# Two-layer hybrid decoder on one core: pools split over the two ends of SBUF, a seventh weight buffer, 384-column blocks second, and the first block's loads and sums in another order

## The chip, the core and the metric

One core of a Trainium2 chip runs the whole program in one launch. The metric is device time in microseconds (us), from one launch to its end. Single times of this kernel lie within about 0.06% of each other.

## What is computed

Two layers; in each, with x of 512 positions by 1024 channels in float32:

```python
for l in range(2):
    x = x + 0.5 * swiglu(rmsnorm(x, ln_ffn1[l]), w_ffn1_gu[l], w_ffn1_down[l])   # 1024 -> 2 x 2816 -> 1024
    h = rmsnorm(x, ln_mix[l])
    u_pool, q, k, v, gate_logits = split(h @ w_in[l])
    a = pool_mixer(u_pool, pool_w[l], pool_scale[l]) @ w_pool_branch[l]
    q, k = partial_rope(rmsnorm(q)), partial_rope(rmsnorm(k))                     # 8 heads, 2 kv heads, 64 wide
    b = swa_sink_attention(q, k, v, sinks[l]) @ w_attn_branch[l]                  # window 128
    x = x + (sigmoid(g_pool) * a + sigmoid(g_attn) * b) @ w_out[l]
    x = x + 0.5 * swiglu(rmsnorm(x, ln_ffn2[l]), w_ffn2_gu[l], w_ffn2_down[l])
```

## The kernel before, in words

Every large product is done with operands split into a high and a low part (ScalarE, called ACT, casts the high part; VectorE, called DVE, subtracts to get the low part), and three matmuls per term: high by high, high by low, low by high. x is held transposed, as eight tiles of 128 channels by 512 positions. A matmul has a stationary operand (loaded by the weight load, `PEld` in the profile) and a moving operand that streams past it; the profile writes `out<-moving,stationary`.

**Feed-forward (`ffn`, four times).** The gate and up projection is done in six blocks of columns, in the order of `GROUPS`: two of 384, two of 512, two of 512. After each pair comes `down`: the pair's rows of the second projection, for all eight output tiles. All blocks but the first of the program run `block`: a Strassen-like scheme with seven products ("a11", "a12", "a22", "s1" to "s4"), each of two chunks of weights. Combinations of activations (T1 to T4) sit in `xgh`/`xgl`, are stationary, and the weights `wh`/`wl` move. The order of products is `ORDER`, or `FIRST` for the first such block of a layer part, where "a11" is followed at once by "a12". After "a11", step `p1` copies the PSUM sums to `r`, because "a12" goes on adding into the same PSUM banks. `open_sums` lets DVE begin the weight sums for "s2". Results are turned by matmuls with the identity (`turned`: transposes into the PSUM banks `pt_tp` and `pt_pv`, then ACT writes `hh` and DVE `hl`); half of them are queued and turned in the next block by `turn`. In `down`, `wh`/`wl` are stationary and `hh`/`hl` move.

The very first block (`plain`) is an ordinary product of 384 columns in two halves j of four chunks. While x is still arriving, `split_plain` and the casts of the weight chunks alternate; `square` and `sums` make the norm; the combinations T1 to T4 (`first`, `others`) are made in the second half.

**Mixer (`mix`, twice).** 20 weight tiles for pool, keys and gates with `xgh`/`xgl` moving, then `br` (moving: `xgh`/`xgl`, where the pool result `ph`/`pl` lies in their spare columns, and the attention result `ah`/`al`) and `out` (moving: `yh`/`yl`). Attention and pooling run beside the gate tiles as generators; `HEADS`, `ATT` and `POOL` say at which half tile t each step of each generator is issued (odd t: after tile t//2 and its `prep`; even t: in the middle of a tile). `heads(b)` rotates q (DVE), transposes q and k into `pt_tp`/`pt_pv` (TensorE, PE), and copies them out to `kT` and `qT` (ACT). `attend` transposes its scores into `pt_tp` at its fourth step, half tile 4 + 3n + 5 for pair n.

**Queues and buffers.** Each engine works strictly in program order. Weights come through `Weights`: `load` issues a chunk's DMA on SyncE (SP) when the buffer six loads back (`RAW`) is free; "s1" and "s3" get a second, adding DMA from GpSimd (POOL). `prep`, after each chunk, makes high parts four chunks ahead and low parts three ahead.

**Addresses.** Pools are stacked upward from byte 8,320 of each partition, in the order they are opened. So, by their sizes, `wh` starts at 38,560, `wl` at 54,944, `xgh` at 83,616, `xgl` at 112,288 (to 140,960), the temporaries (`dh`, `dl` among them) at 145,088, `hh` at 164,672, `hl` at 181,056, `ah` at 179,008, `al` at 187,200, the ring of `yh`/`yl` at 195,648, and the `sums` buffers at 217,920 and 222,016. `pl` for k = 2 and 3 starts at 132,768 and 134,816. `wh`, `wl`, `xgh`, `xgl` start 32 bytes past a multiple of 64, the others named start on a multiple of 64.

Of the kernel before, what the change touches and what calls it, by code (L numbers as in the profile page):

```python
# [24 lines left out]
HT = S // 2  # L25
GROUPS = ((384, 384), (512, 512), (512, 512))
ORDER = ("a11", "s2", "s1", "s3", "a12", "s4", "a22")
# [14 lines left out]
RING = 16  # L42
RAW = 6
HI, LO = 4, 3
WARM = 20
KEYS = (-3,)
NORMS = (-2, -1, 1)
HEADS = ((0, 2, 2), (0, 3, 3), (3, 5, 5), (4, 6, 6))
ATT = tuple(tuple(4 + 3 * n + d for d in (0, 1, 2, 5, 6, 9, 10)) for n in range(8))
# [30 lines left out]


class InOrder:

# [18 lines left out]
def trunk(ctx, tc, xT, consts, vecs, rows, w_g4, w_g3, w_d8, w_d6, w_qkv, w_u, w_pool, w_gate, w_br, w_out, out):  # L102
    nc = Engines(tc)
    pool = lambda name, bufs, **kw: ctx.enter_context(tc.tile_pool(name=name, bufs=bufs, **kw))
    cp, rw, wh_, wl_, xp = pool("cp", 1), pool("rw", RAW), pool("wh", HI), pool("wl", LO), pool("xp", 1)
    tp, sp = pool("tp", TB), pool("sp", 2)
    pa = pool("pa", 1, space=PSUM)
# [43 lines left out]
    class Weights:  # L151
# [3 lines left out]
        def __init__(self):  # L155
            self.plan, self.loads, self.hi, self.lo = [], [], [], []
            self.at = self.loaded = self.summed = 0
            self.sums = None
            for l in range(L):
                for f in range(2):  # L160
                    if f == 1:
                        for kind, src, n in (("u", w_u[l], 2), ("qkv", w_qkv[l], 6), ("u", w_u[l, 2:], 2),
                                             ("gate", w_gate[l], 2 * KT), ("br", w_br[l], KT)):
                            for i in range(n):
                                self.add(kind, CH, src[i])
                        for m in HALVES:
                            self.add("out", CH, w_out[l, m])
                    b = 0
                    for gi, group in enumerate(GROUPS):
                        for i, n in enumerate(group):  # L170
                            w = w_g3[l, f, b] if n == 384 else w_g4[l, f, b - 2]
                            plain = l == f == 0
                            if plain and b == 0:
                                for j in range(2):
                                    for c in range(4):
                                        self.add("plain", 2 * n, w[j, c])
                            else:
                                self.block(w, 2 * n, FIRST if b == int(plain) else ORDER)
                            b += 1
                        last = gi + 1 == len(GROUPS)  # L180
                        for m in (HALVES if f == 1 and last else range(KT)):
                            w = w_d8[l, f, gi - 1, m] if gi else w_d6[l, f, m]
                            self.add("dn", 2 * sum(group) // 2, w)

# [7 lines left out]
        def block(self, w, n, order):  # L192
# [8 lines left out]
            for c in range(2):  # L201
                name["s2", c]["of"] = name["a11", c], name["s1", c]
                name["s4", c]["of"] = name["s2", c], name["a12", c]
                for k in ("a11", "s1", "a12"):
                    name[k, c]["uses"] += 1
            head = [name["s1", c] for c in range(2)]
            rest = [c for c in self.loads[first:] if c is not head[0] and c is not head[1]]
            self.loads[first:] = head + rest
# [45 lines left out]
        def low(self, upto):  # L254
            while len(self.lo) < min(upto, len(self.hi)):
                i = len(self.lo)
                c, n = self.plan[i], self.plan[i]["n"]
                self.lo.append(wl_.tile([P, CH], F32R, name="wl"))
                nc.vector.tensor_tensor(
                    out=self.lo[-1][:, :n], in0=c["raw"][:, :n], in1=self.hi[i].bitcast(F32)[:, :n], op=ALU.subtract  # L260
                )
                c["uses"] -= 1

        def prep(self):
# [55 lines left out]
    class Norm:  # L320
# [5 lines left out]
        def split(self, k, between=lambda: None):  # L326

            g = self.gain[:, k:k + 1]
            if self.h is None:
                self.h = xp.tile([P, 7 * 4 * HT], F32R, name="xgh")  # L330
                self.l = xp.tile([P, 7 * 4 * HT], F32R, name="xgl")
                self.spare = [t[:, KT * S:] for t in (self.h, self.l)]
# [45 lines left out]
        def split_plain(self, k, b12):  # L378
            g = self.gain[:, k:k + 1]
            if self.h is None:  # L380
                self.h, self.l = (
                    xp.tile([P, 7 * 4 * HT], F32R, name=n).rearrange("p (i k t) -> p i k t", i=7, k=4)
                    for n in ("xgh", "xgl")
                )
# [48 lines left out]
    def ffn(ctx, nm, nxt, last):  # L433
        hp = ctx.enter_context(tc.tile_pool(name="hp", bufs=1, reuse_waits="tile"))
        ep = ctx.enter_context(tc.tile_pool(name="ep", bufs=1, reuse_waits="tile"))
        er = ctx.enter_context(tc.tile_pool(name="er", bufs=2, reuse_waits="tile"))
        sums = ctx.enter_context(tc.tile_pool(name="sums", bufs=2, reuse_waits="tile"))
# [12 lines left out]
        def block(n, base, hid, order):  # L450
# [5 lines left out]
            def product(i, b, kind, go):  # L456
# [3 lines left out]
                for c in range(2):  # L460
# [9 lines left out]
                    if c == 0:  # L470
                        W.prep()
                after = go() if go else None
                W.prep()
# [5 lines left out]

            new = lambda name, pool=ep: [pool.tile([P, 512], F32, name=f"{name}{q}")[:, :n] for q in range(2)]  # L480
            r1, sa, u2, v = {}, {}, {}, {}
            rs = lambda b: nm.rstd[:, b:b + 1]

            def p1():
                r1.update(enumerate(new("r", er)))
                each(lambda q: nc.scalar.copy(out=r1[q], in_=pt[1][q]))

            def p2():
# [40 lines left out]
            for kind in order:  # L529
                i, b, go = steps[kind]  # L530
                product(i, b, kind, go)
                if kind in order[:2]:
                    turn()
            turns.extend((r1[q], q, base, n, hid, q) for q in range(2))
# [18 lines left out]
        def plain(n, base, hid):  # L553
# [4 lines left out]
            for k in range(KT):  # L558
                nm.split_plain(k, b12)
                if k % 2 == 0:  # L560
                    W.high(k // 2 + 1)
                    W.low(k // 2 + 1)
            for k in range(KT):
                nm.square(k)
            act = []
            for j in range(2):
                if j:
                    pts = pts[4:] + [pa.tile([P, S], F32, name=name)[:, :n] for name in ("pt_tp", "pt_pv")]
                for c in range(4):
                    wh, wl = (t[:, :2 * n].rearrange("p (k f) -> p k f", k=2) for t in W.take("plain"))  # L570
                    for k in range(2):
                        kt = 2 * c + k
                        for b in range(NB):
# [3 lines left out]
                            ah, al = (t[:, half if kt >= 4 else 0, cols] for t in a)  # L577
                            term(pts[b], kt, KT, ah, al, wh[:, k, :], wl[:, k, :])
                    if j == 0 and c == 3:
                        nm.sums()  # L580
                        for b in range(NB):
# [3 lines left out]
                            )  # L585
                    W.prep()
                    if j:
                        nm.first(c)
                        nm.others(c, nm.scaled(c + 4))
            for b in range(NB):  # L590
                u = (er if b < 2 else ep).tile([P, 512], F32, name=("r0", "r1", "v0", "v1")[b])[:, :n]
                nc.vector.scalar_tensor_tensor(
# [37 lines left out]

        for gi, group in enumerate(GROUPS):
            hid = [hp.tile([P, 8, S], F32R, name=n) for n in ("hh", "hl")]
            base = 0
            for i, n in enumerate(group):
                if nm is first and gi == i == 0:
                    plain(n, base, hid)
                else:
                    fresh = W.sums is None
                    if fresh:
                        open_sums()  # L640
                    block(n, base, hid, FIRST if fresh else ORDER)
                base += n // P
            final = gi + 1 == len(GROUPS)
            if final:
# [4 lines left out]
    @with_exitstack  # L649
    def mix(ctx, l, nm, nxt):  # L650
        mp = ctx.enter_context(tc.tile_pool(name="mp", bufs=1, reuse_waits="tile"))
        rp = ctx.enter_context(tc.tile_pool(name="rp", bufs=RING, reuse_waits="tile"))
        bank["mm"] = ctx.enter_context(tc.tile_pool(name="ps", bufs=4, space=PSUM, reuse_waits="tile"))
# [6 lines left out]
        us = [rp.tile([P, S], F32, name="u", tag="r") for _ in WIN]  # L660
        kv = mp.tile([P, NB, 4, HD], F32, name="kv")
        qT = mp.tile([P, G, S], F32, name="qT")
        kT = mp.tile([P, S], F32, name="kT")
        ph, pl = (t[:, :4 * S].rearrange("p (k t) -> p k t", k=4) for t in nm.spare)
        ah, al = (mp.tile([P, 4, S], F32R, name=n) for n in ("ah", "al"))
        nsink = sp.tile([P, HQ], F32, name="nsink")
# [30 lines left out]
        def rotate(z, n, cos, sin):  # L697
# [6 lines left out]
            nc.vector.tensor_tensor(out=z[..., 0:ROT], in0=ra, in1=rb, op=ALU.add)  # L704

        rs = mp.tile([P, NB, HQ], F32, name="hrs")

        ssq = mp.tile([P, NB, HQ], F32, name="hss")

# [38 lines left out]
        def heads(b):  # L748
# [13 lines left out]
            nc.scalar.copy(out=kT[:, sl], in_=pk[:, :P])  # L762
            nc.scalar.copy(out=qT[:, :, sl], in_=pt.rearrange("p (j t) -> p j t", j=G))
            yield

        def attend(b, jp):
# [8 lines left out]
            for j in range(2):  # L775
                for h, pr in enumerate(group):
                    nc.tensor.matmul(
                        sc[:, 2 * h + j, (0 if b else P):], qT[pr, 2 * jp + j, sl], kT[pr, lo:(b + 1) * P],
                        start=True, stop=True,
# [243 lines left out]
```

## Time and profile before

| | |
|---|---|
| median of 3 runs | 1951.1 us (1950.25 to 1951.4) |
| profiled execution | 1951.35 us, its span 1949.6 us |
| PE busy | 1921.7 us of the span |
| DVE, ACT, POOL busy | 1297.0, 844.3, 82.5 us |
| granted PE clock, mean | 0.995 |

The profile is one execution. Matmuls overlap in it: a matmul's listed duration is longer than the step from its start to the next one's start, so rates are read from starts. Busy time of an engine is the time in which any of its instructions runs. A wait is put down to the engine whose event came last.

### The profile page before, as it was taken

To read this page: it belongs to the slowest core of one execution; us is meant where nothing else is said; L and a number is where in the kernel's file an instruction comes from. 1 tells how busy PE (TensorE), PEld (TensorE's weight loads), DVE (VectorE), ACT (ScalarE), POOL (GpSimd) and SP (SyncE) were. 2 spreads that over 40 slices of the span, in tenths; PEclk is the share of its full clock that TensorE was granted. 3 is DMA by queue.
4 is the path that set the end of the run, shared out by engine and by line. 5 is a ranking of instruction groups with operands and counts; after the bars stand their busy time and mean duration, and the time that the engine had idled before them with its cause. 6 is when DMAs were issued, how large, how long until landed. Compare 5 with 4: busy or idle time off the path is not lost.

```text
span 1949.6 us, 24211 instructions
## 1 busy us (share of the span) xinstructions
PE 1921.7 (99%) x9264; PEld 1617.6 (83%) x9264; DVE 1297.0 (67%) x1896; ACT 844.3 (43%) x1282; POOL 82.5 (4%) x102
## 2 busy tenths in 40 slices
PE   8899999999999999999999999999999999999999
PEld 8788888897788988888889888888877879888887
DVE  5767476666657857648786684765765678575583
ACT  5435244445445534424454442443554455343351
POOL 0000000000000100000010000000000000000000
PEclk9999999999999999999999999999999999999999
DMA  5465563322223666456356655633212237664551
GB/s 184 125 176 168 137 176 120 106 93 77 76 86 77 164 162 182 130 148 176 108 128 164 177 159 121 187 116 100 87 65 86 87 75 185 163 184 141 151 162 44
DMA packets 76628, 256.13 MB, mean 131 GB/s; under 512 B 8640, under 2 KB 8896, under 8 KB 76512
## 3 DMA queue, kind: packets, MB, share of 16 engines
q1 hardware_dynamic: 62928, 209.48, 32.5%
q0 software_dynamic: 13296, 44.71, 13.7%
q8 instruction: 73, 1.20, 0.2%
q10 hardware_dynamic: 288, 0.39, 0.1%
q14 instruction: 43, 0.35, 0.1%
HBM read 252.45 MB, written 2.10 MB: 131 GB/s over the span
## 4 chain that ended last, share of the span: by engine, by line
PE 96%; DVE 2%; DMA 1%; ACT 1%; issue 0%; SPq 0%; ACTq 0%; DVEq 0%; POOLq 0%
PE mm L90 89%; PE sc L90 3%; PE pt_pv L90 2%; PE pt_tp L90 2%; DMA raw<-in_w_g 1%; DVE wl L90 0%; DVE t L90 0%; DVE xgl L90 0%; ACT wh L90 0%; ACT xgh L90 0%; DVE sums L90 0%; DVE r L90 0%; DVE x L90 0%; ACT xg L90 0%; DVE ssq L90 0%
## 5 line engine op out<-in xcount | busy, mean ns | idle before, releaser
L90 ACT CAST wh<-raw 128x1024 fp32r<-128x1024 f32 (+1 forms) x418 | 415.4, 994 | 529.1 <-PE mm L90 490.0
L90 DVE TENSOR_TENSOR wl<-raw,wh 128x1024 fp32r<-128x1024 f32 (+1 forms) x418 | 479.8, 1148 | 130.7 <-PE mm L90 87.6
L90 PE MATMUL mm<-wh,xgh 128*128 128x512 f32 (+2 forms) x1424 | 526.5, 370 | 16.1 <-ACT r L90 10.8
L90 PE MATMUL mm<-wl,xgh 128*128 128x512 f32 (+2 forms) x1424 | 523.7, 368 | 0.3 <-DVE wl L90 0.3
L90 PE MATMUL mm<-wh,xgl 128*128 128x512 f32 (+2 forms) x1424 | 523.6, 368 | 0.0
L90 PEld LDWEIGHTS mm<-wh,xgh 128*128 128x128 f32 x1424 | 270.4, 190 | 52.7 <-ACT r L90 12.2
L90 PEld LDWEIGHTS mm<-wl,xgh 128*128 128x128 f32 x1424 | 270.3, 190 | 35.8 <-DVE wl L90 0.7
L90 PEld LDWEIGHTS mm<-wh,xgl 128*128 128x128 f32 x1424 | 270.1, 190 | 35.0
L90 PE MATMUL mm<-hh,wh 128*128 128x512 f32 x704 | 281.1, 399 | 0.0
L90 PE MATMUL mm<-hl,wh 128*128 128x512 f32 x704 | 279.1, 396 | 0.0
L90 PE MATMUL mm<-hh,wl 128*128 128x512 f32 x704 | 279.0, 396 | 0.0
L90 DVE SCALAR_TENSOR_TENSOR x<-mm,x 128x512 f32<-128x512 f32 x96 | 66.3, 691 | 210.4 <-PE mm L90 210.3
L90 ACT CAST wh<-sums 128x1024 fp32r<-128x1024 f32 (+1 forms) x92 | 90.6, 985 | 173.8 <-PE mm L90 87.9
L90 PEld LDWEIGHTS mm<-hh,wl 128*128 128x128 f32 x704 | 132.6, 188 | 32.4
L90 PEld LDWEIGHTS mm<-hh,wh 128*128 128x128 f32 x704 | 132.6, 188 | 31.2
L90 PEld LDWEIGHTS mm<-hl,wh 128*128 128x128 f32 x704 | 132.6, 188 | 31.1
L90 PE MATMUL mm<-xgh,wh 128*128 128x512 f32 x384 | 154.7, 403 | 0.0
L90 POOL DMA_DIRECT2D raw<-in_w_g x92 | 79.4, 863 | 1773.5 <-DMA raw<-in_w_g 718.2
L90 PE MATMUL mm<-xgh,wl 128*128 128x512 f32 x384 | 150.1, 391 | 0.0
L90 PE MATMUL mm<-xgl,wh 128*128 128x512 f32 x384 | 149.9, 390 | 0.0
L90 DVE TENSOR_TENSOR wl<-sums,wh 128x1024 fp32r<-128x1024 f32 (+1 forms) x92 | 104.3, 1136 | 22.1 <-PE mm L90 22.1
L90 PEld LDWEIGHTS mm<-xgh,wh 128*128 128x128 f32 x384 | 72.1, 188 | 20.0 <-issue 5.6
(203 smaller groups left out, 1981.3 us busy)
## 6 DMA issues: line engine op xcount, KB each, us to landing
raw<-in_w_g SPq DMA_DIRECT2D x160, 512.0 KB, 3.6
raw<-in_w_g POOLq DMA_DIRECT2D x64, 512.0 KB, 6.6
raw<-in_w_d SPq DMA_DIRECT2D x64, 512.0 KB, 3.5
raw<-in_w_g SPq DMA_DIRECT2D x77, 384.0 KB, 3.7
raw<-in_w_gate SPq DMA_DIRECT2D x32, 512.0 KB, 3.5
raw<-in_w_d SPq DMA_DIRECT2D x32, 384.0 KB, 3.1
raw<-in_w_g POOLq DMA_DIRECT2D x28, 384.0 KB, 5.7
raw<-in_w_br SPq DMA_DIRECT2D x16, 512.0 KB, 3.4
```

What stands on the lines that cost most here:

```text
L90: return lambda *args, **kw: self.tc.keep_in_program_order(call(*args, **kw))
```

## The change

- The pools `wh`, `wl`, a new pool `xl` (with `xgh`, `xgl`) are stacked upward first ("left"), all others that live through the program downward from the upper end ("right"). `hp`, `ep`, `sums`, `ap`, `rp` and `mp` follow on the left. By the sizes, `wh` starts at 8,320, `wl` at 24,704, `xgh` at 36,992, `xgl` at 65,664, `hh` and `ah` at 94,336, `hl` at 110,720, `al` at 102,528, the `yh`/`yl` ring at 110,720 (its last six of 16 slots above 131,072). All of these start on a multiple of 64.
- `RAW` is 7. `er` goes: `r` has one buffer instead of two, and `turn` is called before `p1` instead of after it and its `prep`.
- `open_sums` is called at the end of `p1`, behind the copies to `r`, instead of before the block.
- In a `FIRST` block the loads of "a11" come first, then "s1"; before, "s1" came first.
- In all `ffn` but the first the two 384-column blocks come second.
- In `plain`, the first weight chunk is cast in two halves (`parts_of_first`), the norm's `sums` comes one chunk earlier, and the combinations are spread over both halves j (two `first` after each of chunks 0 and 1, then one `others` after each of the next four chunks).
- `qT` is one tile per block of 128 positions with two buffers, and `heads(2)` and `heads(3)` are issued later.

```diff
-RAW = 6
+RAW = 7
-HEADS = ((0, 2, 2), (0, 3, 3), (3, 5, 5), (4, 6, 6))
+HEADS = ((0, 2, 2), (0, 3, 3), (6, 9, 9), (12, 15, 15))
...
+def groups(start):
+    g = [(0, (384, 384)), (768, (512, 512)), (1792, (512, 512))]
+    return g if start else [g[1], g[0], g[2]]
...
-    cp, rw, wh_, wl_, xp = pool("cp", 1), pool("rw", RAW), pool("wh", HI), pool("wl", LO), pool("xp", 1)
-    tp, sp = pool("tp", TB), pool("sp", 2)
+    wh_, wl_, xl = pool("wh", HI, side="left"), pool("wl", LO, side="left"), pool("xl", 1, side="left")
+    cp, rw, xp = pool("cp", 1, side="right"), pool("rw", RAW, side="right"), pool("xp", 1, side="right")
+    tp, sp = pool("tp", TB, side="right"), pool("sp", 2, side="right")
...
-            head = [name["s1", c] for c in range(2)]
+            head = [name[k, c] for k in (("a11", "s1") if order is FIRST else ("s1",)) for c in range(2)]
...
+        def parts_of_first(self, k):
+            c = self.plan[0]
+            if k == 0:
+                self.hi.append(wh_.tile([P, CH], F32R, name="wh"))
+                self.lo.append(wl_.tile([P, CH], F32R, name="wl"))
+            cols = slice(k * c["n"] // 2, (k + 1) * c["n"] // 2)
+            split(self.hi[0][:, cols], self.lo[0][:, cols], c["raw"][:, cols])
+            c["uses"] -= k * 2
...
-        er = ctx.enter_context(tc.tile_pool(name="er", bufs=2, reuse_waits="tile"))
...
+                if kind in order[:2]:
+                    turn()
                 after = go() if go else None
                 W.prep()
...
             def p1():
-                r1.update(enumerate(new("r", er)))
+                r1.update(enumerate(new("r")))
                 each(lambda q: nc.scalar.copy(out=r1[q], in_=pt[1][q]))
+                if W.sums is None:
+                    open_sums()
...
                 product(i, b, kind, go)
-                if kind in order[:2]:
-                    turn()
...
                 nm.split_plain(k, b12)
-                if k % 2 == 0:
+                if k < 2:
+                    W.parts_of_first(k)
+                elif k % 2 == 0:
                     W.high(k // 2 + 1)
                     W.low(k // 2 + 1)
...
+            combos = [lambda j=j: nm.first(j) for j in range(4)]
+            combos += [lambda j=j: nm.others(j, nm.scaled(j + 4)) for j in range(4)]
...
+                    if j == 0 and c == 2:
+                        nm.sums()
+                    W.prep()
+                    for _ in range(2 if j == c // 2 == 0 else 1):
+                        if combos:
+                            combos.pop(0)()
                     if j == 0 and c == 3:
-                        nm.sums()
...
-                    W.prep()
-                    if j:
-                        nm.first(c)
-                        nm.others(c, nm.scaled(c + 4))
...
-                    fresh = W.sums is None
-                    if fresh:
-                        open_sums()
-                    block(n, base, hid, FIRST if fresh else ORDER)
+                    block(n, base, hid, FIRST if W.sums is None else ORDER)
...
-        qT = mp.tile([P, G, S], F32, name="qT")
+        qp = ctx.enter_context(tc.tile_pool(name="qp", bufs=2, reuse_waits="tile"))
+        qT = {}
...
+            qT[b] = qp.tile([P, G, P], F32, name="qT")
-            nc.scalar.copy(out=qT[:, :, sl], in_=pt.rearrange("p (j t) -> p j t", j=G))
+            nc.scalar.copy(out=qT[b], in_=pt.rearrange("p (j t) -> p j t", j=G))
```

More of the change, by code (lines that the diff above doesn't have):

```diff
@@ L25 @@
 HT = S // 2
-GROUPS = ((384, 384), (512, 512), (512, 512))
 ORDER = ("a11", "s2", "s1", "s3", "a12", "s4", "a22")
@@ L167, in __init__ @@
                             self.add("out", CH, w_out[l, m])
-                    b = 0
-                    for gi, group in enumerate(GROUPS):
+                    plain = l == f == 0
+                    for gi, (at, group) in enumerate(groups(plain)):
                         for i, n in enumerate(group):
-                            w = w_g3[l, f, b] if n == 384 else w_g4[l, f, b - 2]
-                            plain = l == f == 0
-                            if plain and b == 0:
+                            w = w_g4[l, f, (at - 768) // 512 + i] if at else w_g3[l, f, i]
+                            if plain and gi == i == 0:
                                 for j in range(2):
@@ L177, in __init__ @@
                             else:
[L178 to L183, printed above, removed]
+                                self.block(w, 2 * n, FIRST if 2 * gi + i == int(plain) else ORDER)
+                        for m in (HALVES if f == 1 and gi == 2 else range(KT)):
+                            w = w_d8[l, f, at // 1024, m] if at else w_d6[l, f, m]
+                            self.add("dn", sum(group), w)
         def add(self, kind, n, src=None, more=None, of=None):
@@ L205, in block @@
                     name[k, c]["uses"] += 1
-            head = [name["s1", c] for c in range(2)]
-            rest = [c for c in self.loads[first:] if c is not head[0] and c is not head[1]]
+            head = [name[k, c] for k in (("a11", "s1") if order is FIRST else ("s1",)) for c in range(2)]
+            rest = [c for c in self.loads[first:] if not any(c is h for h in head)]
             self.loads[first:] = head + rest
@@ L329, in split @@
             if self.h is None:
-                self.h = xp.tile([P, 7 * 4 * HT], F32R, name="xgh")
-                self.l = xp.tile([P, 7 * 4 * HT], F32R, name="xgl")
+                self.h = xl.tile([P, 7 * 4 * HT], F32R, name="xgh")
+                self.l = xl.tile([P, 7 * 4 * HT], F32R, name="xgl")
                 self.spare = [t[:, KT * S:] for t in (self.h, self.l)]
@@ L381, in split_plain @@
                 self.h, self.l = (
-                    xp.tile([P, 7 * 4 * HT], F32R, name=n).rearrange("p (i k t) -> p i k t", i=7, k=4)
+                    xl.tile([P, 7 * 4 * HT], F32R, name=n).rearrange("p (i k t) -> p i k t", i=7, k=4)
                     for n in ("xgh", "xgl")
@@ L478, in each @@
                 return [make(q) for q in range(2)]
-            new = lambda name, pool=ep: [pool.tile([P, 512], F32, name=f"{name}{q}")[:, :n] for q in range(2)]
+            new = lambda name: [ep.tile([P, 512], F32, name=f"{name}{q}")[:, :n] for q in range(2)]
             r1, sa, u2, v = {}, {}, {}, {}
@@ L585, in plain @@
                             )
-                    W.prep()
-                    if j:
-                        nm.first(c)
-                        nm.others(c, nm.scaled(c + 4))
             for b in range(NB):
-                u = (er if b < 2 else ep).tile([P, 512], F32, name=("r0", "r1", "v0", "v1")[b])[:, :n]
+                u = ep.tile([P, 512], F32, name=("r0", "r1", "v0", "v1")[b])[:, :n]
                 nc.vector.scalar_tensor_tensor(
@@ L629, in down @@
                 done(m, pd)
-        for gi, group in enumerate(GROUPS):
+        for gi, (_, group) in enumerate(groups(nm is first)):
             hid = [hp.tile([P, 8, S], F32R, name=n) for n in ("hh", "hl")]
@@ L637, in ffn @@
                 else:
-                    fresh = W.sums is None
-                    if fresh:
-                        open_sums()
-                    block(n, base, hid, FIRST if fresh else ORDER)
+                    block(n, base, hid, FIRST if W.sums is None else ORDER)
                 base += n // P
-            final = gi + 1 == len(GROUPS)
+            final = gi == 2
             if final:
@@ L650, in mix @@
     def mix(ctx, l, nm, nxt):
+        ap = ctx.enter_context(tc.tile_pool(name="ap", bufs=1, reuse_waits="tile"))
+        ah, al = (ap.tile([P, 4, S], F32R, name=n) for n in ("ah", "al"))
+        rp = ctx.enter_context(tc.tile_pool(name="rp", bufs=RING, reuse_waits="tile"))
         mp = ctx.enter_context(tc.tile_pool(name="mp", bufs=1, reuse_waits="tile"))
-        rp = ctx.enter_context(tc.tile_pool(name="rp", bufs=RING, reuse_waits="tile"))
         bank["mm"] = ctx.enter_context(tc.tile_pool(name="ps", bufs=4, space=PSUM, reuse_waits="tile"))
@@ L660, in mix @@
         us = [rp.tile([P, S], F32, name="u", tag="r") for _ in WIN]
-        kv = mp.tile([P, NB, 4, HD], F32, name="kv")
-        qT = mp.tile([P, G, S], F32, name="qT")
+        rs = mp.tile([P, NB, HQ], F32, name="hrs")
+        ssq = mp.tile([P, NB, HQ], F32, name="hss")
+        qp = ctx.enter_context(tc.tile_pool(name="qp", bufs=2, reuse_waits="tile"))
+        qT = {}
         kT = mp.tile([P, S], F32, name="kT")
         ph, pl = (t[:, :4 * S].rearrange("p (k t) -> p k t", k=4) for t in nm.spare)
-        ah, al = (mp.tile([P, 4, S], F32R, name=n) for n in ("ah", "al"))
+        kv = mp.tile([P, NB, 4, HD], F32, name="kv")
         nsink = sp.tile([P, HQ], F32, name="nsink")
@@ L704, in rotate @@
             nc.vector.tensor_tensor(out=z[..., 0:ROT], in0=ra, in1=rb, op=ALU.add)
-        rs = mp.tile([P, NB, HQ], F32, name="hrs")
-        ssq = mp.tile([P, NB, HQ], F32, name="hss")
         def sums(z, out):
@@ L777, in attend @@
                     nc.tensor.matmul(
-                        sc[:, 2 * h + j, (0 if b else P):], qT[pr, 2 * jp + j, sl], kT[pr, lo:(b + 1) * P],
+                        sc[:, 2 * h + j, (0 if b else P):], qT[b][pr, 2 * jp + j, :], kT[pr, lo:(b + 1) * P],
                         start=True, stop=True,
```

## The prediction

> **What bounds the kernel.** I read the page's busy times and chain first, then PE's list of waits, then the groups of matmuls by shape, then starts in the timeline.
>
> ```profile
> span 1949.6 us, 24211 instructions
> PE 96%; DVE 2%; DMA 1%; ACT 1%; issue 0%; SPq 0%; ACTq 0%; DVEq 0%; POOLq 0%
> ```
> ```profile
> PE mm L90 <- ACT r L90: 10.8, 4, 3.2
> PE pt_tp L90 <- DVE v L90: 6.4, 1, 6.4
> PE mm L90 <- ACT wh L90: 5.2, 1, 5.2
> ```
>
> PE is the chain: 96% of it. PE's waits come to about 24 us, nearly all in six places, and only the one at the very start has a transfer behind it. So two things can move the time: the step from one matmul to the next, and those six places.
>
> ```profile
> L90 PE MATMUL mm<-wh,xgh 128*128 128x512 f32 x896 | 350.0, 391 | 0.0
> ...
> L90 PE MATMUL mm<-hh,wh 128*128 128x512 f32 x704 | 281.1, 399 | 0.0
> ...
> L90 PE MATMUL mm<-xgh,wh 128*128 128x512 f32 x384 | 154.7, 403 | 0.0
> ...
> L90 PE MATMUL mm<-wh,xgh 128*128 128x384 f32 x432 | 149.3, 346 | 16.1 <-ACT r L90 10.8 <-ACT wh L90 5.2
> ...
> L90 PE MATMUL mm<-yh,wh 128*128 128x512 f32 x128 | 50.8, 397 | 0.0
> ...
> L90 PE MATMUL mm<-ah,wl 128*128 128x512 f32 x64 | 25.4, 398 | 0.0
> ```
>
> These give the counts (each stands three times: high by high, high by low, low by high). Listed durations overlap, so the step comes from starts. One tile of `br` holds the clean contrast:
>
> ```profile
> 544.76 0.39 PE L90 MATMUL mm<-xgh,wh 128*128 128x512 f32 x1
> ...
> 547.48 0.40 PE L90 MATMUL mm<-ah,wh 128*128 128x512 f32 x1
> ...
> 550.29 0.39 PE L90 MATMUL mm<-xgh,wh 128*128 128x512 f32 x1
> ```
>
> Twelve matmuls with `xgh`/`xgl` moving take 2.72 us, 226.7 ns a step; the next twelve, same shape, same weights, `ah`/`al` moving, take 2.81 us, 234.2 ns. All that differs is where the moving operand lies. Each step with `hh`, `hl`, `yh` or `yl` moving is like the second kind.
>
> **The change, part by part.**
>
> *1. Place of the operands.* 704 + 128 + 64 = 896 matmuls, times three = 2688 steps, at 7.5 ns (the difference above): 20.2 us, all on the path. But is it the place, and which property of it? The 128 KB line itself fits badly: `pl` for k = 2 and 3 starts at 132,768 and 134,816, above 131,072, and lies in the fast dozen. And a stationary operand costs too:
>
> ```profile
> 33.72 0.33 PE L90 MATMUL mm<-wh,xgh 128*128 128x384 f32 x1
> ...
> 34.76 0.34 PE L90 MATMUL pt_tp<-wh,sums 128*128 128x384 f32 x1
> ...
> 35.83 0.33 PE L90 MATMUL mm<-wh,xgh 128*128 128x384 f32 x1
> ```
>
> Six steps with `wh` moving and `xgh`/`xgl` stationary take 1.04 us (173.3 ns), six with the same `wh` moving and `sums` (at 217,920) stationary 1.07 us (178.3 ns). Three properties fit all these rows: a line near 140 KB for either operand; moving and stationary standing differently against multiples of 64 bytes (every slow pair has one on a multiple and one 32 bytes past it); or any operand on a multiple of 64. After the change all large operands lie under 143.5 KB and all on multiples of 64, so by the first two all pairs are fast, by the third all are slow. I take the gain; the third is a rival. A few steps are lost after each break by transposes, so I take 19.5 us. Bounds: nothing to 20.2, or a loss as below.
>
> [...]
>
> *2. Three later `ffn` starts.* One of three alike:
>
> ```profile
> 638.07 0.34 PE L90 MATMUL mm<-wh,xgl 128*128 128x384 f32 x1
> 641.62 0.69 PE L90 MATMUL mm<-wh,xgh 128*128 128x384 f32 x1 [3.22 <-ACT r L90]
> ...
> 644.96 0.34 PE L90 MATMUL mm<-wl,xgh 128*128 128x384 f32 x1
> ```
> ```profile
> 637.89 0.63 ACT L90 ACTIVATE sq<-x 128x512 f32<-128x512 f32 x1
> 640.36 0.83 ACT L90 CAST wh<-sums 128x768 fp32r<-128x768 f32 x1 [1.84 <-DVE sums L90]
> 641.10 0.85 ACT L90 COPY r<-mm 128x384 f32<-128x384 f32 x2
> ```
> ```profile
> L90 DVE TENSOR_TENSOR wl<-raw,wh 128x1024 fp32r<-128x1024 f32 (+1 forms) x418 | 479.8, 1148 | 130.7 <-PE mm L90 87.6
> ```
> ```profile
> 641.60:645.00 3.40, 3.38 (x11) 3.38 (x12) 1.28 (x2) 1.19 (x2) 0.86 (x1) 0.51 0.65 213
> ```
>
> "a12" waits for ACT's copies to `r`; ACT holds them behind `wh<-sums`, which waits for DVE's sum, and DVE is still at the norm. The gap costs 3.55 - 0.17 = 3.4 us. Then the granted clock is 0.51: ten matmuls in 3.34 us instead of 1.73, 1.6 more. With `open_sums` behind the copies, ACT can copy `r` as `sq` ends (638.5), and a 512-column "a11" ends 24 x (226.7 - 173.3) = 1.3 us later, at about 639.5: no gap. Late next are the sums of "s2" (DVE, about 1.15 us each, like a low part, and behind the norm): sum, cast, low part end about when "a12" does. I leave 0.2 us and take 3 x 4.8 = 14.4. Bounds: 0 to 15.
>
> [...]
>
> *3. The first 65 us.*
>
> ```profile
> 9.86 0.83 ACT L90 CAST wh<-raw 128x768 fp32r<-128x768 f32 x1 [5.18 <-DMA raw<-in_w_g]
> ```
> ```profile
> 19.80 5.46 DVE L90 TENSOR_TENSOR ssq<-ssq,sq 128x512 f32<-128x512 f32 x7
> ...
> 31.70 0.16 DVE L90 TENSOR_SCALAR rs_v<-pt_tp 128x4 f32<-128x4 f32 x1 [4.11 <-PE pt_tp L90]
> ...
> 33.88 0.16 DVE L90 SCALAR_TENSOR_TENSOR rstd<-rs_t,rstd 128x4 f32<-128x4 f32 x1
> ```
> ```profile
> 37.76 0.42 DVE L90 TENSOR_TENSOR d<-x 128x256 f32<-128x256 f32 x1
> ...
> 39.37 0.48 DVE L90 SCALAR_TENSOR_TENSOR t<-x,vec,xg 128x256 f32<-128x256 f32 x1
> ...
> 42.01 0.95 DVE L90 TENSOR_TENSOR wl<-raw,wh 128x768 fp32r<-128x768 f32 x1
> ```
> ```profile
> 57.37 1.14 DVE L90 SCALAR_TENSOR_TENSOR r<-mm,rstd,sa 128x384 f32<-128x384 f32 x2
> ```
> ```profile
> 52.35 0.34 PE L90 MATMUL mm<-wh,xgl 128*128 128x384 f32 x1
> 59.09 0.90 PE L90 MATMUL pt_tp<-cst,r 128*128 128x128 f32 x3 [6.40 <-DVE v L90]
> ```
>
> The halved first cast lets PE begin some 4 us sooner, but the norm's `sums` now stands a chunk earlier and PE must wait there for the squares (25.3), then at `pt_tp` until DVE reads the sums behind four `first`. So I expect "a11" to end near 52.3, as now. DVE is what counts: a `first` takes 1.6 us, an `others` 2.6, a low part 0.9, the norm's chain 2.4 with its start. From 25.3: four `first`, one low, the norm's chain, then four times low and `others`, two lows, and two results and a bit for `v` (1.7): 6.4 + 0.9 + 2.4 + 14.0 + 1.8 + 1.7 = 27.2, so 52.5 instead of 59.0. Then `turn` before the copies: transposes, two `hh` casts, the first copy of `r`, some 2 us, so "a12" at 54.4 instead of 61.8. With the slow-clock steps (1.4) gone and 0.4 for late sums: 7.4 + 1.4 - 0.4 = 8.4 us. Bounds: 3 to 10.
>
> *4. `heads(2)` and `heads(3)`.* At half tiles 9 and 15 they now meet the transposes of `attend` 0 and 2 in `pt_tp`:
>
> ```profile
> 432.44 0.60 PE L90 MATMUL pt_tp<-cst,q 128*128 128x128 f32 x4
> ...
> 432.91 0.47 PE L90 MATMUL mm<-xgh,wh 128*128 128x512 f32 x1
> ```
> ```profile
> 432.41 1.05 ACT L90 CAST wh<-raw 128x1024 fp32r<-128x1024 f32 x1 [1.78 <-PE mm L90]
> 433.37 0.26 ACT L90 COPY kT<-pt_pv 128x128 f32<-128x128 f32 x1
> 433.52 0.59 ACT L90 COPY qT<-pt_tp 128x512 f32<-128x512 f32 x1
> ```
>
> This is `heads(1)` now: PE goes on at 432.91, ACT has emptied `pt_tp` at 434.11, behind the weight cast. With `attend`'s transposes next in PE's queue, PE waits 1.2 us, and all gate tiles behind it. Four times: 5 us lost. Bounds: 0 to 7.
>
> *5. The rest.* The seventh buffer, the loads' order, 384 columns second, `turn` before `p1` in later blocks, one `r`: nothing. Their cover is that PE waits for no weights after the start; DVE is the engine that would show if it went: a low part late by its own length costs PE up to 1.15 us. Moves within DMA queues likewise: SP and POOL only issue loads.
>
> Sum, against this execution's 1951.35 us (span 1949.6, 0.25 above the median): 1951.35 - 19.5 - 14.4 - 8.4 + 5.0 = 1914.05. I say 1914.
>
> **The rivals.**
>
> *A: the place is not what costs*; the slow steps belong to the kind of stage. For: each slow kind has its own stage. Against: `br` alternates within one tile. 1914 + 19.5 = 1933.5. [...]
>
> *B, slower: multiples of 64 bytes are what costs.* Every slow row has such an operand and no fast one does; after the change all do. Then 896 + 384 matmuls with 512 columns, times three, at 7.5 ns (28.8) and 432 x 3 with 384 at 5.0 (6.5) slow down by 35.3 us, and the old slow ones stay: 1951.35 + 35.3 - 14.4 - 8.4 + 5.0 = 1968.9. It decides once these 5,136 steps lose more than 3.5 ns each (17.8 us over 5,136). Against: it makes the better aligned start the dearer one.
>
> *C: the waits are replaced.* ACT's copies of `r` now stand behind `turn` and late sums behind the copies; if half of parts 2 and 3 comes back: 1914 + 11.4 = 1925.4.
>
> **How the numbers follow.** My forecast 0.60 (own range 1904 to 1922: parts 3 and 4 at their bounds), C 0.13, A 0.17, B 0.10. Range 1902 to 1935: it takes in A and C and leaves B out. Faster by over 0.2% (about 4 us, the least this kernel's measurement tells from no change): the forecast, C and most of A, 0.87; same 0.03; slower 0.10.
>
> **What would show it.** Part 1: twelve steps of `ah` in 2.72 us, and the `hh` group's mean below 395 ns; if `xgh` steps go to 234, B. Part 2: no row "PE mm <- ACT r" over 1 us, and a clock of 1.00 at each `ffn` start. Part 3: first transposes of `r` near 52.5. Part 4: PE's waits list `pt_tp <- ACT qT`, four times, over 1 us each. What would make it wrong: B, or DVE falling behind in the 512-column blocks that now follow the norm.

## The result and the profile after

The changed kernel takes 1919.69 us, the median of four runs (1918.39 to 1920.03); the kernel before takes 1951.19 us beside it (1950.25 to 1951.4). The ratio is 0.9838, 95% interval 0.9821 to 0.9855: 31.5 us less. The profiled execution is the fastest of the four, 1918.39 us; the working below goes by it. The kernel before was also run seven times beside each batch of the experiments below: its medians there lie between 1949.87 and 1951.69 us, and the seven times of one batch up to 3.0 us apart, more than its first three. So a single time, or a comparison across batches, tells nothing below some 3 us.

The head of the page after, its busy times, and the line of the chain:

```profile
span 1916.6 us, 24198 instructions
...
PE 1897.8 (99%) x9264; PEld 1611.6 (84%) x9264; DVE 1296.1 (68%) x1897; ACT 843.2 (44%) x1283; POOL 82.5 (4%) x102
...
PE 95%; DVE 2%; ACT 1%; DMA 1%; issue 0%; SPq 0%; DVEq 0%
```

PE's list of waits after (sum, times, longest, in us):

```profile
PE pt_tp L95 <- ACT qT L95: 9.2, 4, 3.5
PE mm L95 <- ACT wh L95: 2.6, 1, 2.6
PE pt_pv L95 <- DVE warm_in L95: 1.1, 1, 1.1
PE pt_tp L95 <- DVE ssq L95: 1.0, 1, 1.0
PE mm L95 <- ACT r L95: 0.9, 1, 0.9
```

The two big rows of before (`r`, 10.8 us, and `v`, 6.4 us) are gone but for one copy of `r`. The longest wait is a new one, of `pt_tp` for `qT`. The groups of matmuls by shape:

```profile
L95 PE MATMUL mm<-wh,xgh 128*128 128x512 f32 x896 | 350.5, 391 | 0.0
...
L95 PE MATMUL mm<-hh,wh 128*128 128x512 f32 x704 | 276.3, 392 | 0.0
...
L95 PE MATMUL mm<-wh,xgh 128*128 128x384 f32 x432 | 146.5, 339 | 3.5 <-ACT wh L95 2.6 <-ACT r L95 0.9
...
L95 PE MATMUL mm<-yh,wh 128*128 128x512 f32 x128 | 49.8, 389 | 0.0
...
L95 PE MATMUL mm<-ah,wl 128*128 128x512 f32 x64 | 24.9, 389 | 0.0
```

`hh`, `yh` and `ah` as moving operands now cost what `wh` always did. In the timeline, of the tile of `br` that held the contrast (between the rows shown stand the other products of each dozen):

```profile
541.13 0.39 PE L95 MATMUL mm<-ah,wh 128*128 128x512 f32 x1
...
543.85 0.39 PE L95 MATMUL mm<-xgh,wh 128*128 128x512 f32 x1
...
546.57 0.39 PE L95 MATMUL mm<-ah,wh 128*128 128x512 f32 x1
```

Both dozens take 2.72 us, 226.7 ns a step.

Bookkeeping of the profiled execution, from starts. The steps with `hh`/`hl` moving sum to 496.43 us before and 481.32 after, `yh`/`yl` 89.97 and 87.04, `ah`/`al` 44.90 and 43.52: 19.4 us less. The first `down` starts 9.2 us sooner (the first start in the two rows below). Each of the three later `ffn` starts lost 3.4 us idle and some 1.6 in the slow clock before, and has no gap now: 14.9 less. The waits for `qT` cost 11 more. Together 32.5; the two executions differ by 33.0, so 0.5 us is left unassigned.

The `hh` group by tile, before and after (minimum, median and longest duration in ns, first and last start in us):

```profile
L90 PE MATMUL mm<-hh,wh x704: 392/397/482, 89.4 to 1945.0; 128*128 128x512 f32 x176
```
```profile
L95 PE MATMUL mm<-hh,wh x704: 388/389/477, 80.2 to 1912.0; 128*128 128x512 f32 x176
```

### The profile page after: what moved, and what is told of

It is laid out like the page before. It is cut to its first block, busy times and chain, and to the rows that moved or that the text cites. A ratio compares the mean times of both kernels' runs of the same rounds, so it can differ in the third digit from the quotient of the medians.

```text
span 1916.6 us, 24198 instructions
## 1 busy us (share of the span) xinstructions
PE 1897.8 (99%) x9264; PEld 1611.6 (84%) x9264; DVE 1296.1 (68%) x1897; ACT 843.2 (44%) x1283; POOL 82.5 (4%) x102
## 4 chain that ended last, share of the span: by engine, by line
PE 95%; DVE 2%; ACT 1%; DMA 1%; issue 0%; SPq 0%; DVEq 0%
PE mm L95 89%; PE sc L95 2%; PE pt_pv L95 2%; PE pt_tp L95 2%; ACT s L95 1%; DMA raw<-in_w_g 1%; DVE wl L95 0%; DVE m L95 0%; DVE s L95 0%; DVE ssq L95 0%; ACT wh L95 0%; DVE win L95 0%; DVE nm L95 0%; DVE z L95 0%; ACT qT L95 0%
## 5 line engine op out<-in xcount | busy, mean ns | idle before, releaser
L95 ACT CAST wh<-raw 128x1024 fp32r<-128x1024 f32 (+2 forms) x419 | 414.8, 990 | 491.2 <-PE mm L95 459.1
L95 DVE TENSOR_TENSOR wl<-raw,wh 128x1024 fp32r<-128x1024 f32 (+2 forms) x419 | 480.3, 1147 | 113.9 <-PE mm L95 73.7
L95 PE MATMUL mm<-hh,wh 128*128 128x512 f32 x704 | 276.3, 392 | 0.0
L95 PE MATMUL mm<-hh,wl 128*128 128x512 f32 x704 | 274.3, 390 | 0.0
L95 PE MATMUL mm<-hl,wh 128*128 128x512 f32 x704 | 274.0, 389 | 0.0
```

Source lines behind the costliest of these rows:

```text
L95: return lambda *args, **kw: self.tc.keep_in_program_order(call(*args, **kw))
```

## The experiments

### Which property of the place costs

Three pads shift `hh`, `ah`, the rings and `sums`, and leave `wh`, `wl`, `xgh`, `xgl` where the change put them. The floats per partition are 8, 16 and 32, which is 32, 64 and 128 bytes:

```diff
     wh_, wl_, xl = ...
     cp, rw, xp = ...
     tp, sp = ...
+    pad = pool("pad", 1, side="left").tile([P, 8], F32, name="pad")    # 16, 32
+    nc.gpsimd.memset(pad, 0.0)
```

The fourth kernel is the one before, with a pad that leaves everything high and only makes `hh`, `hl`, `ah`, `al` (and the `yh` ring, 256 bytes off by 512) stand like `wh`:

```diff
     tp, sp = pool("tp", TB), pool("sp", 2)
     pa = pool("pa", 1, space=PSUM)
+    pad = pool("pad", 1).tile([P, 216], F32, name="pad")
+    nc.gpsimd.memset(pad, 0.0)
```

32 bytes:

> The changed kernel with 32 unused bytes between xgl and the pools after it, so that hh, hl, ah, al, yh, yl lie 32 bytes higher, all still low, and 32 bytes past a multiple of 64 while wh, wl and xgh stay on one. If a line in the address decides (theory P), the steps with hh moving stay at 227 ns and the time at 1919 us. If the relative stand of moving and stationary operand decides (theory R), they go to 234 ns: 2688 x 7.5 ns = 20 us more, 1939 us.

64 bytes:

> The same with 64 unused bytes. Theory P: 1919 us. Theory R with a period of 64 bytes: 1919 us too, steps of 227 ns; theory R with a period of 128 bytes or more: 234 ns and 1939 us.

128 bytes:

> The changed kernel with 128 unused bytes in front of hh and the pools after it. 32 bytes made the hh steps 234 ns, 64 bytes some 230, and in the older layout 256 bytes (yh) left them at 227. If the period of the relative stand is 128 bytes: steps of 227 ns and 1919 us. If it is 256: slow steps again, 1927 us or more.

The kernel before, matched:

> The kernel before with 864 unused bytes behind its lasting pools: hh, hl, ah, al and the sums buffers stay high (165,536 and up) but now start 32 bytes past a multiple of 64 and at the same place in every 2 KB as wh, wl, xgh; yh and yl differ from wh by 256 bytes in every 512. Theory P: no change, 1951 us. Theory R: 2304 steps of hh, hl, ah, al go from 234 to 227 ns, 17 us less, 1934 us; the 384 steps of yh, yl go with them (2.9 us more) if the period is 256 bytes or a part of it.

| kernel | `hh` starts at | minus `wh`, modulo 256 | mean `hh`/`hl` step | us |
|---|---|---|---|---|
| before | 164,672 | 160 | 235.2 ns | 1951.19 |
| after | 94,336 | 0 | 228.0 | 1919.69 |
| pad of 32 | 94,368 | 32 | 234.3 | 1936.95 (one time) |
| pad of 64 | 94,400 | 64 | 229.9 | 1927.24 (one time) |
| pad of 128 | 94,464 | 128 | 234.0 | 1937.53 (one time) |
| before, matched | 165,536 | 0 | 227.9 | 1932.67 (1931.56 to 1932.71) |

(The mean of an undisturbed stretch is about 1 ns lower, since the `hh` steps contain the breaks.) The groups by tile, first of the kernel with the 32-byte pad, then of the matched one:

```profile
L95 PE MATMUL mm<-ah,wh x64: 394/396/400, 543.7 to 1541.2; 128*128 128x512 f32 x64
...
L95 PE MATMUL mm<-hh,wh x704: 393/396/485, 79.5 to 1930.6; 128*128 128x512 f32 x176
```
```profile
L90 PE MATMUL mm<-ah,wh x64: 389/389/390, 543.5 to 1536.7; 128*128 128x512 f32 x64
...
L90 PE MATMUL mm<-hh,wh x704: 388/389/477, 89.4 to 1926.4; 128*128 128x512 f32 x176
...
L90 PE MATMUL mm<-yh,wh x128: 388/389/390, 584.3 to 1580.2; 128*128 128x512 f32 x128
```

A shift of 32 bytes gives the loss back, far below 128 KB; the same operands at 165,536 and above are fast as soon as they stand like their partners. So it is not the height of the address, and not a line at 128 KB. (The trace after says the same by itself: the last six slots of the `yh` ring lie above 131,072, and no `yh` matmul in any slot is over 390 ns.) What counted in these six kernels is how the moving and the stationary operand stand to each other. The 128-byte pad is slow (234.0 ns), and the `yh` ring of the matched kernel, 256 bytes off, is fast (its matmuls last 389 ns in the median, against 397 before): this fits a period of 256 bytes. At 64 bytes neither of the two forecasts came (227 or 234 ns): the mean lies between, because two of every three steps take 229 to 232 ns (medians), while the third, with the low part `hl` or `yl` moving, stays at 226 (`yl` lasts 388 ns in the mean there, `yh` 394 and 392). The matched kernel against before: ratio 0.991 (0.9893 to 0.9926), 17.2 us below the kernel before beside it (1949.87), and 18.6 between the two profiled executions; by its steps 19.6, but its profile has more slow clock (0.992 in the mean, against 0.995). The pad of 32 adds 17.3 us to the changed kernel, and its steps with `hh`, `yh`, `ah` 13.3 + 2.6 + 1.3 = 17.2.

### The transposes of `heads(2)` and `heads(3)` in other banks

```diff
-            pt = pa.tile([P, S], F32, name="pt_tp")
+            pt = mm() if b > 1 else pa.tile([P, S], F32, name="pt_tp")
...
-            pk = pa.tile([P, S], F32, name="pt_pv")
+            pk = mm() if b > 1 else pa.tile([P, S], F32, name="pt_pv")
```

> The changed kernel with the transposes of heads(2) and heads(3) going to banks of the ring mm instead of pt_tp and pt_pv, so that the transposes of attend need not wait for ACT's copies. The four waits for ACT's copy to qT (9.2 us) should go, and the slow-clock stretch after one of them (about 1.7 us): 1909 us. If the wait turns up elsewhere (for mm, or for kT at the next product with v): 1914 us or more.

1906.57 us (1906.05 to 1907.29), ratio 0.9778 to the kernel before (0.9763 to 0.9792). The interval lies wholly below the change's own (0.9821 to 0.9855): of the kernels here this is the fastest, 13.1 us below the change in medians; as the kernel before was 1.3 us faster in this batch too, the 11.1 us between the two profiled executions is the better figure. Its waits list, from the top:

```profile
PE mm L95 <- ACT wh L95: 2.9, 1, 2.9
PE pt_pv L95 <- DVE warm_in L95: 1.1, 1, 1.1
```

The waits for `qT` are gone, and so is the stretch of slow clock behind the second of them. The windows view, the changed kernel's stretch behind that wait, and the same times here (busy time of PE, PEld, DVE, ACT, POOL, then granted clock, DMA share, GB/s):

```profile
465.40:469.00 3.60, 3.60 (x11) 3.02 (x12) 2.32 (x5) 1.28 (x4) 0.00 (x0) 0.53 0.41 135
```
```profile
465.40:469.00 3.60, 3.60 (x20) 2.70 (x17) 1.48 (x5) 2.09 (x6) 0.00 (x0) 1.00 0.45 146
```

### `open_sums` back ahead of the block

```diff
-                if W.sums is None:
-                    open_sums()
...
-                    block(n, base, hid, FIRST if W.sums is None else ORDER)
+                    fresh = W.sums is None
+                    if fresh:
+                        open_sums()
+                    block(n, base, hid, FIRST if fresh else ORDER)
```

> The changed kernel with open_sums back in front of the FIRST block, the rest as changed. If the order on ACT is what closed the gaps at the later ffn starts, they return: three waits of PE for ACT's r, each with a slow-clock stretch. With 512-column blocks a11 lasts 1.3 us longer than before, but the sums are longer too: 3 x 4 us, 1931 us. If the 512-column block alone had closed them: 1919 us.

1934.14 us (one time), 14.4 more than the change. The waits list and one of the places:

```profile
PE mm L95 <- ACT r L95: 10.6, 4, 2.8
```
```profile
635.90 0.50 PE L95 MATMUL mm<-wh,xgh 128*128 128x512 f32 x1 [2.75 <-ACT r L95]
```

The gaps are back, 3.13 us between starts at three `ffn` starts and 2.67 in the first. Of the 15.8 us between the two profiled executions, 11.9 come at the three later starts, 2.4 before the first `down` (82.57 instead of 80.20 us), and the rest, 1.5 us, in a slow-clock stretch of the second mixer (granted clock 0.995 in the mean, against 0.997 in the change). So it is the place of `open_sums` in ACT's queue that closes them.

### 384 columns first in every `ffn`

```diff
-    return g if start else [g[1], g[0], g[2]]
+    return g
```

> The changed kernel with the 384-column blocks first in every ffn, as before the change. My step 5 says nothing: 1919 us. The rival: with 384 columns a11 ends 1.3 us sooner, before ACT has copied r, and a wait of up to 1.3 us returns at each of three ffn starts: 1923 us.

1921.35 us (1919.93 to 1923.35), ratio 0.9844 (0.9827 to 0.986): not to be told from the change.

```profile
PE mm L95 <- ACT r L95: 2.5, 4, 0.9
```
```profile
631.10 0.44 PE L95 MATMUL mm<-wh,xgh 128*128 128x384 f32 x1 [0.53 <-ACT r L95]
```

The trace still shows what the order is for: half a microsecond at each of the three starts, which the longer "a11" of 512 columns covers. That is 1.6 us of the 14.9, under what the times can tell.

### The seventh buffer, and the order of the first loads

Six buffers with the changed order of loads, and six with the order of before:

```diff
-RAW = 7
+RAW = 6
```
```diff
-RAW = 7
+RAW = 6
...
-            head = [name[k, c] for k in (("a11", "s1") if order is FIRST else ("s1",)) for c in range(2)]
+            head = [name[k, c] for k in ("s1",) for c in range(2)]
```

Buffer alone:

> The changed kernel with six raw buffers, its new order of loads kept. With six buffers and the old order the time was 1925.9 us. If the missing buffer makes the late low parts at the ffn starts: some 1925 us again, the same six waits for DVE's low part. If the order of the loads made them: 1920 us.

Buffer and order:

> The changed kernel with six raw buffers and s1 ahead of a11 in the loads, both as before the change. My step 5 says nothing: 1919 to 1920 us. The rival: at the ffn starts the 512-column loads come late without them, and PE's waits list a cast or a low part waiting for a transfer, 1 us or more at each of three starts: 1923 us or more.

1924.68 us (1922.92 to 1925.78), ratio 0.9863 (0.9847 to 0.9879), and 1925.86 us (1925.47 to 1926.44), ratio 0.9872 (0.9855 to 0.9888). The runs of either lie above all of the change's (at most 1920.03), by 5.0 and 6.2 us in medians, though the intervals of the ratios overlap. With six buffers and the changed order, PE's waits and, in the timeline, ACT and PE at a start of `ffn`:

```profile
PE mm L95 <- DVE wl L95: 4.1, 7, 0.8
```
```profile
644.14 1.05 ACT L95 CAST wh<-raw 128x1024 fp32r<-128x1024 f32 x1 [7.22 <-DMA raw<-in_w_g]
...
653.77 0.50 PE L95 MATMUL mm<-wl,xgh 128*128 128x512 f32 x1 [0.42 <-DVE wl L95]
```

With six buffers a chunk's load arrives late, ACT casts it late (at 644.14, after 7.2 us of waiting for the transfer), DVE's low parts, which need these casts, and the sums between them then come one behind the other, and PE catches up with them in the later half of the first 512-column block (it runs from 624.75 to 664.4 us here). Six of the seven waits come in this block, at each of the three later `ffn` starts. Most of the loss comes with the buffer; the order of the loads (1.2 us between the two, in different batches) is not resolved.

### The first 65 us, part by part

The combinations back in the second half:

```diff
-                    for _ in range(2 if j == c // 2 == 0 else 1):
-                        if combos:
-                            combos.pop(0)()
+                    if j:
+                        combos[c]()
+                        combos[c + 4]()
```

> The changed kernel with the combinations back in the second half of the plain block, one first and one others after each of its chunks; the norm's sums stay a chunk earlier. If DVE's late work was the 6.4 us wait, PE waits for v again, 5 to 7 us, with a slow-clock stretch after it: 1926 us. If the earlier start of the kernel alone had closed it: 1919 us.

The norm's sums a chunk later, as before:

```diff
-                    if j == 0 and c == 2:
+                    if j == 0 and c == 3:
```

> The changed kernel with the norm's sums after chunk 3 again, the combinations spread as changed. The wait for the squares (1.0 us) goes, but the sums then stand behind one more others on DVE, and PE, which needs pt_tp in the second half, waits for them some 3 to 5 us: 1921 to 1924 us. The rival: the earlier place only costs, and without it the time falls to 1917 us.

The first chunk cast in one piece:

```diff
-                if k < 2:
-                    W.parts_of_first(k)
-                elif k % 2 == 0:
+                if k % 2 == 0:
```

> The changed kernel with the first weight chunk cast whole again. PE should then begin near 10.7 us instead of 5 us. My step 3 says that the earlier start is given back in the waits for the squares and for pt_tp, so the second block's a12 starts within 1.5 us of where it does now (53.8 us), 1920 us. The rival: the early start is kept, and without it everything is 4 us later: 1924 us.

One time each: 1928.75, 1925.33 and 1921.06 us. The line of PE's waits that tells each, in this order:

```profile
PE pt_tp L95 <- DVE v L95: 5.5, 1, 5.5
```
```profile
PE pt_tp L95 <- DVE rs_v L95: 5.3, 1, 5.3
```
```profile
PE mm L95 <- ACT wh L95: 5.5, 1, 5.5
```

And the slow clock that follows the first of them:

```profile
57.30:64.00 6.70, 5.41 (x18) 4.99 (x19) 5.49 (x8) 3.39 (x6) 0.00 (x0) 0.50 0.26 73
```

With the combinations in the second half, DVE is late with `v` as in the kernel before, and PE's clock is at half for two stretches: the first `down` starts at 88.28 us instead of 80.20, 8.1 us later. With the norm's sums a chunk later PE waits for DVE's `rs_v` earlier on, and the first `down` starts at 83.47, 3.3 us later; the rest of the 5.6 us above the median comes in slow-clock stretches of the two mixers (granted clock 0.995 in the mean, against 0.997), which this edit does not touch. With the first chunk cast whole PE's products start at 10.25 us; in the changed kernel they start at 5.13, and PE then waits 2.6 us behind 7.57. At the end one time shows no difference (1.4 us above the median), and "a12" starts at 54.1 instead of 53.84 us, the first `down` at 80.41 instead of 80.20: the early start is given back in waits.

## Why the prediction came out as it did

The forecast was 1914 us in 1902 to 1935, faster at 0.87; measured 1919.69. The mechanisms it named were those that act, and one term of the sum had the wrong size. The time lies inside the likeliest case's own range, 1904 to 1922, near its upper end. (That range's lower end does not follow from the bounds it names: parts 3 and 4 at their best give 1907.5.)

*Step 1, place of the operands: right.* 19.5 predicted, 19.4 measured. Of the three properties that it could not tell apart, the line near 140 KB falls (matched kernel), and so does "any operand on a multiple of 64", rival B: `wh` and `xgh` both stand on one now and the group stays at 391 ns. What is left is the second, the two operands standing differently, but it was drawn too narrowly: the pads of 64 and 128 bytes keep both on multiples of 64 and still cost, and 256 is the period that fits. Rival A (no place costs, 1933.5) falls too: the pad of 32 bytes alone takes 17.3 us.

*Step 2, the later `ffn` starts: right.* 14.4 predicted, 14.9 measured, and the kernel with `open_sums` put back loses 11.9 of it at these starts (one of its three gaps has no slow clock behind it, and "a11" is longer there). The 0.2 us that I left at each start did not come. The list shows one "PE mm <- ACT r" row, 0.9 us, under the 1 us named as the sign. Rival C fails here.

*Step 3, the first 65 us: right.* The path was foreseen: the early start is given back in waits, DVE decides. PE waited 2.6 us for the next cast behind 7.57 and 1.0 us for the squares behind 22.85; I had named the second, not the first, and the later wait that I had named as well, at `pt_tp` until DVE has read the sums, did not come. Two slow-clock stretches of 3.4 us, at 11.56 and 25.21 (granted clock 0.50 in both), I had not named either. They did not count: with 384 columns first in every `ffn` the profile has no slow stretch in the first 65 us, and there "a12" starts at 53.98. The return of PE:

```profile
51.82 0.55 PE L95 MATMUL pt_tp<-cst,r 128*128 128x128 f32 x3
...
53.84 0.45 PE L95 MATMUL mm<-wh,xgh 128*128 128x384 f32 x1 [0.95 <-ACT r L95]
```

Predicted 52.5 and 54.4. To the first `down` 9.2 us were won, predicted 8.4.

*Step 4, `heads(2)` and `heads(3)`: the term that was mis-sized.* Predicted 5.0 as four times 1.2 us; measured 9.2 us of waits, and 11 with the slow clock, above the bound of 7 that I gave it. The place, the engine and the four times are right. PE's timeline after, at half tile 15 of the first layer:

```profile
461.21 0.60 PE L95 MATMUL pt_tp<-cst,q 128*128 128x128 f32 x4
461.64 0.27 PE L95 MATMUL pt_pv<-cst,kv 128*128 128x128 f32 x1
...
465.40 1.03 PE L95 MATMUL pt_tp<-cst,s 128*128 128x128 f32 x4 [3.49 <-ACT qT L95]
```

And ACT in the same stretch:

```profile
461.14 0.49 ACT L95 ACTIVATE s<-s,nm,scale 128x128 f32<-128x128 f32 x1 [3.70 <-DVE nm L95]
...
463.16 0.60 ACT L95 CAST dh<-d 128x512 fp32r<-128x512 f32 x1
463.67 1.04 ACT L95 CAST wh<-raw 128x1024 fp32r<-128x1024 f32 x1
464.61 0.26 ACT L95 COPY kT<-pt_pv 128x128 f32<-128x128 f32 x1
464.77 0.58 ACT L95 COPY qT<-pt_tp 128x512 f32<-128x512 f32 x1
```

I took ACT's queue from `heads(1)`, where only a weight cast stands ahead of the copies; that holds at half tile 9 (1.1 us). At half tile 15 the queue still holds what was issued half a tile before: a step of attention, four exponentials that had waited for DVE's `nm` until 461.14, and a pooling cast `dh`. So it is 461.14 to 465.35 before `qT` is out, and two of the four waits are 3.5 us. I had read what these instructions cost, but not which generators issue just ahead of that place. In the first layer the granted clock was then 0.53 over 3.6 us, which I had priced for the `ffn` starts and not here. The kernel that moves these transposes to other banks wins 11.1 us by the profiles (13.1 in medians), where I had named 5.0.

*Step 5, "the rest nothing": half right.* 384 columns second and the loads' order are within what the times tell. The seventh buffer is not nothing: without it the change loses 5.0 us. I had named the cover (PE waits for no weights) and the engine that shows if it goes (DVE, a low part late by up to 1.15 us), but I priced the buffer against the kernel before, where 384-column blocks come first. In the order of the change the cover needs the buffer; which part of the new order makes it so is not shown, since six buffers were not run with the 384-column blocks first. In the sum the zero stood rightly, since buffer and order come together. `turn` ahead of `p1` and the single `r` were not run apart.

The errors against 1914.05 add up to 0.5 + 0.8 better and 0.1 + 6 worse, so 1918.9; the profiled execution took 1918.39.

## What to carry to other kernels

Where matmuls of one shape step at two rates in one trace, compare early on where the moving and the stationary operand start modulo 256 bytes, the period that fits here: a pad of a few bytes is a cheap edit, and it tells (32 bytes cost 17.3 us). A copy's price is what stands ahead of it in its engine's queue at that very place (PE waited 1.1 us for `qT` at half tile 9, 3.5 us at half tile 15), so list the instructions of every generator that issues there or just ahead, and do not take the price from a quieter place. A buffer priced at nothing against the order before can be what the new order rests on.

## What the runs showed of the hardware that I had not expected

- The step of a 512-column float32 matmul with a weight load of its own went, in the six kernels of the table, with where the moving operand stands relative to the stationary one: 226.7 ns where they differ by a multiple of 256 bytes and 234.2 at 160 bytes off (the `ah` dozens of after and before); with `hh`/`hl` moving, breaks included, 228.0 at 0, 234.3 at 32, 229.9 at 64, 234.0 at 128 and 235.2 at 160. Why is open: no run here looked at the weight load and the moving stream by themselves.
- In the profiles of before and after, the granted clock falls to 0.50 in stretches of 3.41 us, once of 6.83 (before, at 57.81 us); the last of either, 2.80 and 2.44 us, is cut short by the end. The length of a gap alone did not decide whether it cost a stretch: 3.76 us between starts in the first layer of the changed kernel was followed by half the clock, the same 3.76 us in the second layer was not (0.50 and 1.00 in the last row of each fence below); with `open_sums` ahead of the block the gap of 3.13 us at 977.1 us was followed by a slow stretch (steps of 0.43 us), the one at 632.8 was not (0.23). The stretches of one execution start whole multiples of 3.413 us apart (after: (465.53 - 11.56) / 133 = 3.413; before: (641.49 - 57.81) / 171 = 3.413 and (993.07 - 57.81) / 274 = 3.413), so their starts give a grid, and the two gaps of 3.76 us lie differently on it (windows view, columns as above):

```profile
462.12:465.53 3.41, 0.13 (x1) 0.13 (x2) 1.74 (x3) 3.23 (x10) 0.00 (x0) 1.00 0.00 0
465.53:468.94 3.41, 3.41 (x11) 2.83 (x12) 2.19 (x5) 1.28 (x4) 0.00 (x0) 0.50 0.42 136
```
```profile
1407.61:1411.02 3.41, 1.79 (x11) 1.31 (x9) 1.85 (x7) 2.39 (x10) 0.00 (x0) 1.00 0.27 109
1411.02:1414.44 3.42, 1.55 (x9) 1.37 (x10) 3.12 (x6) 2.17 (x6) 0.00 (x0) 1.00 0.00 0
1414.44:1417.85 3.41, 3.41 (x21) 2.09 (x19) 0.72 (x2) 0.93 (x4) 0.00 (x0) 1.00 0.47 154
```

  In the first layer PE is busy for 0.13 us of one cell of the grid, and half the clock follows; in the second layer the gap is shared by two cells, busy for 1.79 and 1.55 us, and the clock stays. In the profiles of before and after, between 60 and 1900 us, half the clock followed each of the four full-clock cells in which PE idled for 2.5 us or more (before 3.09, 2.66 and 2.50 us, in the cells from 638.08, 989.65 and 1600.64; after 3.28, in the cell from 462.12), and none in which it idled less (1.87 at most). So what goes with the clock here is how much of a gap falls in one cell, not its whole length. In the first 25 us after, a cell with 0.96 us of idle (from 21.80) was followed by half the clock too; why is open.
